# Group 1's operands ahead of the context's, and later turns of the token groups, in a hybrid gated-recurrence and convolution layer

## Chip, cores and metric

The kernel runs on one core of one Trainium2 chip. The metric is the device time of an execution in microseconds. "PE" is TensorE's matmul row, "PEld" its weight loads, "DVE" VectorE, "ACT" ScalarE, "POOL" GpSimd and "SP" SyncE, whose queue issues the DMAs named here. Times are in microseconds from the span's start unless stated otherwise.

## The reference

One layer of a flow-matching generator: batch 1, 2048 tokens and 256 context tokens of width 1024. Cut to what matters:

```python
shift, scale, gate = jnp.split(jax.nn.silu(c) @ w_ada[l] + b_ada[l], 3, axis=-1)
shift_c, scale_c, gate_c = jnp.split(jax.nn.silu(c_ctx) @ w_ada[l] + b_ada[l], 3, axis=-1)
h = rmsnorm(x, norm_w[l]) * (1.0 + scale[:, None]) + shift[:, None]
hc = rmsnorm(xc, norm_w[l]) * (1.0 + scale_c) + shift_c
p = h @ w_in[l]                      # 1024 x 9216 columns
pc = hc @ w_in[l, :, :HG_COLS]
...
qc, vc, kcf, gcf, kcb, gcb = hgrn_prep(pc[..., :HG_COLS], lb_f, lb_b)
oc, s_f, s_b = bidir_scan(qc, kcf, kcb, vc, gcf, gcb, s0, s0)
q, v, kf, gf, kb, gb = hgrn_prep(p[..., :HG_COLS], lb_f, lb_b)
o, _, _ = bidir_scan(q, kf, kb, v, gf, gb, s_f, s_b)
y_hg = hgrn_out(o, p[..., 4 * HG_WIDTH:HG_COLS], hg_onorm_w[l], x.dtype)
y_cv = conv_branch(p[..., HG_COLS:], conv_w[l], grid=True)
y = jnp.concatenate([y_hg, y_cv], axis=-1) @ w_out[l]
x = x + gate[:, None] * y
return rmsnorm(x, final_norm_w)
```

Everything is float32. The context gives only the start states of each head's scan, one per direction.

## The kernel before

**Products.** A float32 operand is split into a high and a low float16 part, and a product takes three matmuls (hi by hi, hi by lo, lo by hi). The input projection works on *units*: a pair of 128-column blocks of `w_in` against one group of 512 tokens (four groups, NG = 4). A normal unit ("head") goes by a scheme of seven block products (`seven`, matmuls at L890 to L892) in place of eight, for which a group needs seven operands, B11, T1, T2, B21, T3, B22 and T4 (`OPS`), made from the rows of h by additions and subtractions. Two kinds of units are simpler: "plain" (L1410 to L1412), for group 0's first use, straight from its rows, and "ctx" (L1396 to L1398), for the 256 context tokens, from the tile `hc`.

**Stretches.** The work runs in stretches, one for each head and group. Head 0 takes the groups in the order 0, 1, 2, 3 (stretches 0 to 3), head 1 in the order 3, 2, 1, 0 (stretches 4 to 7), and so on. Stretch 0 has four plain units and the context's three units of head 0; stretches 1 to 3 have the head units for gates and values and one unit of output gates. In a stretch, `run` issues the matmuls of its units one step (three matmuls) after the other, and between them the other work: the scan of the stretch before (`chain`: levels, key turns, states, outputs) and `extra`. Each piece of that work has a weight, and `merge_steps` spreads the two lists over the stretch's steps by their weights. So the order on every engine is written out by the program, and each engine works its instructions off in that order.

**How a group's operands come to be.** `norm_group` gives a group five lists: loads; squares (L238) and the norm (`rsqrt`, thirteen small DVE instructions, then scaling at L244 on ACT and L246 on DVE); four *turns*; four *late turns*; and `raw`. A turn k transposes blocks k and k + 4 of the normed rows on PE (L253), applies scale and shift on ACT (L274), and in `combine` makes the seven operands' slices: four subtractions on DVE (L328, L329, L331, L337), high parts by `cast` (L281 on ACT, L279 on POOL), low parts on DVE (L298), into "pair" tiles of which there are four, and seven stores on SP (L300) into `Hd`, the group's operands in DRAM. `prefetch` loads an operand back into a "hop" tile (L1297) when a slot is free and the group is said to be ready (`set_ready`); a stretch's first product needs the first of these, hop1B for stretch 1.

**Group 0** is special. Its rows are transposed early, between the products of the modulation (`modulate`, L200), as `raw` rows; when the modulation's result `pada` is there, `modulate_end` copies it (L209), transposes it (L212) and adds the bias, `affine` makes scale and shift for the tokens (m = 0) and the context (m = 1) with one small matmul each (L139), and group 0's rows are scaled (L268, L270), cast (L281) and subtracted (L290) into `plain`. The scaled rows are also stored to `Xd` (L313). Three of group 0's operands are slices of `plain` and are stored by `store_first` (L1333, twelve stores); the other four are made by `late_turn`, which loads rows back from `Xd` (L321).

**When.** The lists are joined at L1445 to L1463. In stretch 0, `early` is the context's norm and turns, then group 1's norm and turns, then group 2's norm and its first turn. Stretch 1 has the other three turns of group 2, then the loads, the norm and the first turn of group 3; stretch 2 has group 3's other three; stretch 3 has group 0's four late turns. The context's scan steps stand in stretch 1.

## Time and profile before

| | us |
|---|---|
| median of 3 runs | 2189.02 (2188.14 to 2189.62) |
| the profiled execution | 2194.8 |
| its span | 2193.0 |
| PE busy | 2095.4 (96%) |
| DVE busy | 1652.7 (75%) |
| ACT busy | 1168.0 (53%) |
| POOL busy | 158.2 (7%) |

The stretches begin, by their first matmul, at 44.7 (stretch 0), 97.0 (1), 154.3 (2), 195.2 (3), 238 (4), 281.9 (5) and 314.9 (6). A row of a timeline has the start, the duration, engine, line, operation and tiles, and in brackets the idle time of the engine before it with what ended it. A row of a window has, for each engine, busy time and the number of instructions; then the granted clock of TensorE, where 1.00 is full speed, the mean busy share of the DMA engines, and GB/s. A row of a group has busy time, the mean in ns, and the idle time before its members.

### The profile page before, as it was taken

The numbers are of one execution on the slowest core, as the hardware profiler recorded it, in microseconds if no ns is written. First come the engines' busy times: TensorE is split into PE (matmuls) and PEld (weight loads), VectorE is DVE, ScalarE is ACT, GpSimd is POOL, SyncE is SP. The second block draws the span as 40 slices with busy tenths as digits, with TensorE's granted clock in tenths as the row PEclk, the third lists the DMA queues.
The fourth block names the chain that finished last, engine by engine and source line by source line (L and its number), as shares of the span: only waits on it lengthen the run. The fifth ranks groups of instructions, "written<-read, shape, count | busy, mean of one in ns | idle before, by whom it ended". The sixth has DMA issues, their size and how long they took to land.

```text
span 2193.0 us, 51887 instructions
## 1 busy us (share of the span) xinstructions
PE 2095.4 (96%) x21563; PEld 1469.7 (67%) x21563; DVE 1652.7 (75%) x3457; ACT 1168.0 (53%) x2340; POOL 158.2 (7%) x239
## 2 busy tenths in 40 slices
PE   5789999999999999999999998999999999999998
PEld 2677788888888888888888887444444444444443
DVE  7887887878769777788687786688778646687775
ACT  7865656656557555575676654354444323333332
POOL 0211100010101110110111100000000000000000
PEclk8999999999999999999999999999999999999999
DMA  9765533342344233423543357933443215633321
GB/s 348 237 210 177 158 99 107 136 136 88 99 140 143 96 112 107 141 97 124 187 152 129 117 183 232 292 106 111 135 139 96 92 32 181 212 118 114 124 88 58
DMA packets 196176, 309.89 MB, mean 141 GB/s; under 512 B 13538, under 2 KB 126562, under 8 KB 194148
## 3 DMA queue, kind: packets, MB, share of 16 engines
q1 hardware_dynamic: 193780, 302.64, 42.2%
q8 instruction: 169, 2.77, 0.5%
q10 hardware_dynamic: 2160, 3.93, 0.5%
q14 instruction: 67, 0.55, 0.1%
HBM read 241.50 MB, written 65.01 MB: 140 GB/s over the span
## 4 chain that ended last, share of the span: by engine, by line
PE 66%; DVE 19%; ACT 7%; DMA 5%; issue 2%; POOL 1%; SPq 0%; POOLq 0%; ACTq 0%; DVEq 0%
PE sa L890 8%; PE sa L892 8%; PE sa L891 8%; PE sb L890 4%; PE sb L891 4%; PE sb L892 4%; PE sa_o L890 2%; PE sa_o L891 2%; PE sa_o L892 2%; DVE e_p L152 2%; PE A L599 2%; PE sc L890 2%; PE sc L892 2%; PE sc L891 2%; DVE Q L460 2%
## 5 line engine op out<-in xcount | busy, mean ns | idle before, releaser
L453 DVE TENSOR_TENSOR K<-K,tot 128x512 f32<-128x512 f32 x192 | 133.6, 696 | 61.8 <-PE A L627 27.6
L890 PEld LDWEIGHTS <-e_p 128*128 128x128 f16 x1368 | 134.3, 98 | 63.1 <-issue 5.2
L891 PEld LDWEIGHTS <-e_p 128*128 128x128 f16 x1368 | 134.5, 98 | 61.6 <-issue 12.3
L892 PEld LDWEIGHTS <-e_p 128*128 128x128 f16 x1368 | 134.5, 98 | 52.9 <-issue 1.5
L460 DVE TENSOR_TENSOR Q<-Q,tot 128x512 f32<-128x512 f32 x192 | 132.4, 690 | 41.4 <-PE A L599 28.0
L569 ACT ACTIVATE km<-K 128x512 f32<-128x512 f32 x160 | 109.0, 686 | 72.1 <-DVE K L453 63.0
L890 PEld LDWEIGHTS <-whib_p 128*128 128x128 f16 x912 | 89.7, 98 | 44.1 <-issue 7.5
L891 PEld LDWEIGHTS <-whib_p 128*128 128x128 f16 x912 | 89.8, 98 | 39.7 <-issue 5.7
L891 PEld LDWEIGHTS <-whia_p 128*128 128x128 f16 x912 | 89.5, 98 | 37.3 <-issue 4.8
L890 PEld LDWEIGHTS <-whia_p 128*128 128x128 f16 x912 | 89.5, 98 | 37.2 <-DMA hop3B<-Hd3B 2.4
L892 PEld LDWEIGHTS <-wlob_p 128*128 128x128 f16 x912 | 89.8, 98 | 35.0 <-issue 0.6
L892 PEld LDWEIGHTS <-wloa_p 128*128 128x128 f16 x912 | 89.6, 98 | 34.6
L151 ACT ACTIVATE e_p<-ws_p,sc_p 128x512 f16<-128x512 f32 x108 | 77.2, 717 | 51.4 <-DVE ws_p L413 32.0
L576 POOL COPY qm<-Q 128x512 f32<-128x512 f32 x64 | 55.6, 869 | 622.0 <-DVE Q L460 619.0
L635 POOL COPY A<-Ac 32x128 f32<-32x128 f32 x128 | 68.4, 534 | 375.0 <-ACT A L631 371.0
L897 ACT ACTIVATE u<-sa,sx_w 128x256 f32<-128x256 f32 (+1 forms) x114 | 59.7, 523 | 58.6 <-PE sa L892 49.0
L897 ACT ACTIVATE p<-sb,sx_w 128x256 f32<-128x256 f32 (+1 forms) x114 | 59.3, 520 | 54.8 <-PE sb L892 54.0
L897 ACT ACTIVATE p<-sa,sx_w 128x256 f32<-128x256 f32 (+1 forms) x114 | 59.0, 517 | 47.1 <-PE sa L892 46.2
L813 ACT ACTIVATE cv<-c,small 128x512 f32<-128x512 f32 (+1 forms) x36 | 24.2, 673 | 105.8 <-DVE c L831 49.9
L152 DVE SCALAR_TENSOR_TENSOR e_p<-ws_p,sc_p,e_p 128x512 f16<-128x512 f32 x108 | 78.7, 748 | 0.4 <-ACT e_p L151 0.4
L378 ACT ACTIVATE junk<-ws_p 128x1024 f16<-128x1024 f32 x72 | 75.6, 1050 | 1.9 <-DMA ws_p<-in_w_in 1.8
L151 ACT ACTIVATE hiS_o<-y_o,sc_y 128x1024 f16<-128x1024 f32 x32 | 36.7, 1148 | 74.3 <-PE sa_o L891 32.1
(865 smaller groups left out, 6978.9 us busy)
## 6 DMA issues: line engine op xcount, KB each, us to landing
ws_p<-in_w_in SPq DMA_DIRECT2D x72, 512.0 KB, 4.3
y_o<-yT SPq DMA_DIRECT2D x32, 512.0 KB, 3.7
xt_x<-in_x SPq DMA_DIRECT2D x16, 512.0 KB, 5.1
wa<-in_w_ada SPq DMA_DIRECT2D x16, 512.0 KB, 10.2
Gd<-zs SPq DMA_DIRECT2D x32, 256.0 KB, 3.6
wos<-in_w_out SPq DMA_DIRECT2D x32, 256.0 KB, 3.8
sg<-Gd SPq DMA_DIRECT2D x32, 256.0 KB, 4.1
yT<-y SPq DMA_DIRECT2D x32, 256.0 KB, 2.2
```

The source lines that it names most:

```text
L151: S.activation(hi, src, AF.Copy, scale=st[:, 0:1])
L152: V.scalar_tensor_tensor(lo, src, st[:, 0:1], hi, ALU.mult, ALU.subtract)
L378: S.activation(junk.rearrange("p (k n) -> p k n", k=KT), stage[i], AF.Abs, accum_out=r)
L453: V.tensor_tensor(m, m, sub(cur, nb + 1, [[2, np_], [-(nb + 1), 2], [0, B]]), ALU.mult)
L460: V.tensor_tensor(m, m, sub(cur, 1, [[2, np_], [nb - 1, 2], [0, B]]), ALU.mult)
L569: S.activation(sub(s.km, 0, [[2 * B, n // (2 * B)], [B, 2], [1, B]]), mix(s.K, n, B, n // (2 * B)), AF.Copy)
L576: G.tensor_copy(sub(qm, 0, [[2 * B, n // (2 * B)], [B, 2], [1, B]]), mix(s.qf, n, B, n // (2 * B)))
L635: G.tensor_copy(A3[js, :, js], s.Ac[js])
L890: PE.matmul(ps, hi[:, k], rh, start=start and k == 0, stop=False, skip_group_check=not start)
L891: PE.matmul(ps, hi[:, k], right(name, 1, k), start=False, stop=False, skip_group_check=not start)
L892: PE.matmul(ps, lo[:, k], rh, start=False, stop=k == nk - 1, skip_group_check=not start)
L897: last_keep.append(S.activation(r, ps, AF.Copy, scale=sx))
```

## The change

- `modulate_end` copies `pada` half on DVE and half on ACT. The last two of group 0's eight `raw` transposes no longer stand ahead of it: they are issued behind its transposes, in banks of another pool, and are copied by ACT. `follow` holds an instruction behind a given one on the same engine.
- Group 1's loads stand ahead of the context's. `affine(1)` comes behind the first three low parts of group 0; a group's squares come behind the last cast, and its norm behind the last low part, of the group named by `before`.
- Stretch 0 keeps only its four plain units. `early` is now an empty step of weight 25.0, group 1's norm and turns, group 0's `store_first`, and group 2's norm. The context's norm and turns (with a third of their weights), its three units and, behind most of the scan of group 0, its scan steps are in stretch 1.
- Stretch 1 has all four turns of group 2 and, behind them, group 3's loads and norm; stretch 2 has all four turns of group 3.
- Group 0's four late turns leave stretch 3: two are in stretch 4 and two in stretch 5.

```diff
     def modulate_end(pada):
         ada_r = ring("ada_r")
-        V.tensor_copy(ada_r, pada)
+        V.tensor_copy(ada_r[:, :HW], pada[:, :HW])
+        S.activation(ada_r[:, HW:], pada[:, HW:], AF.Copy)
...
+    def follow(marks, fn):
+
+        if not marks:
+            return fn()
+        with tc.issue_after(marks[-1].ins):
+            fn()
...
+        before = None if first_ops is not None else "x1" if m else f"x{row0 // GW - 1}"
...
         def square(i):
-            S.activation(junk, xs[i], AF.Square, accum_out=ssq[:, i:i + 1])
+            follow(casts.get(before), lambda: S.activation(junk, xs[i], AF.Square, accum_out=ssq[:, i:i + 1]))
 
         def norm():
+            follow(lows.get(before), scaled)
...
             if wi == 0:
...
-                          (vk, "plain", 1, sg_.value_in), (vk, "plain", 2, sg_.query_in),
-                          (zk, "ctx", 1, lambda ps, w, c_=c_: c_.gate_in(0, ps, w)),
-                          (zk, "ctx", 2, lambda ps, w, c_=c_: c_.gate_in(1, ps, w)), (vk, "ctx", 1, c_.value_in)]
+                          (vk, "plain", 1, sg_.value_in), (vk, "plain", 2, sg_.query_in)]
...
-                if i == 0:
+                if i == 0 or wi == 1:
                     units += [(zk, "ctx", 1, lambda ps, w, c_=c_: c_.gate_in(0, ps, w)),
                               (zk, "ctx", 2, lambda ps, w, c_=c_: c_.gate_in(1, ps, w))]
+                if wi == 1:
+                    units.append((vk, "ctx", 1, c_.value_in))
...
-            chain += scan_steps(heads[pa_h], heads[pa_h].segs[pi])
+            scan = scan_steps(heads[pa_h], heads[pa_h].segs[pi])
+            chain += scan[:-2] + context_steps(h) + scan[-2:] if wi == 1 else scan
...
-    for _, st in ctx_norm[0] + x1_norm[0]:
+    for _, st in x1_norm[0] + ctx_norm[0]:
         st()
-    modulate_end(pada)
+    turned = modulate_end(pada)
+    for k in (KT - 2, KT - 1):
+        follow(turned, first[4][k])
     affine(0, 7)
     for _, st in first[2]:
         st()
-    affine(1, 7)
+    follow(lows["x0"][:3], lambda: affine(1, 7))
...
-            early = (ctx_norm[1] + ctx_norm[2] + n1[1] + n1[2] if wi == 0 else n1[2][1:]) + ready_
+            early = [paced(25.0, lambda: None)] + n1[1] + n1[2] + ready_ if wi == 0 else n1[2] + ready_
             if wi == 0:
                 more_params()
                 for _, st in n2[0]:
                     st()
-                early += [paced(0.1, store_first)]
+                early += [paced(0.1, store_first), paced(0.1, lambda: next_w(1, 6))]
+            if wi == 1:
+                early = [paced(w_ / 3, fn_) for w_, fn_ in ctx_norm[1] + ctx_norm[2]] + early
             if n2 is not None:
-                early += [paced("pause", lambda: None)]
-                if wi == 0:
-                    early += [paced(0.1, lambda: next_w(1, 6))]
-                else:
-                    early += n2[0]
-                early += n2[1] + n2[2][:1]
+                early += ([paced("pause", lambda: None)] + n2[0] if wi else []) + n2[1]
             extra = early + extra
-        elif wi == NG - 1:
-            extra = first[3] + extra
+        elif wi in (NG, NG + 1):
+            extra = first[3][(wi - NG) * 2:(wi - NG) * 2 + 2] + extra
```

On PE, at the end of stretch 0, the last turn of group 1 (its rows are `xt_x_414` and below), the context's products (from `hc`) and the first transposes of group 2 (`xt_x_487` and on) stood ahead of the first product from hop1B. Before:

```order
L253 MATMUL xT_x_951<-ident,xt_x_414 128x128
L1396 MATMUL u_937<-hc,whia_p_218 128x256
...
L1398 MATMUL u_1122<-hc,wloa_p_276 128x256
L253 MATMUL xT_x_1081<-ident,xt_x_487 128x128
...
L253 MATMUL xT_x_1180<-ident,xt_x_489 128x128
L890 MATMUL sa_1163<-hop1B_1012,whia_p_218 128x256
```

At the same place now (group 1's rows end with `xt_x_396`, the context's are `xt_c_398` and `xt_c_400`, group 2's end with `xt_x_494`):

```order
L268 MATMUL xT_x_819<-ident,xt_x_396 128x128
L1425 MATMUL u_796<-hop_2_151,whib_p_277 128x256
...
L535 MATMUL vt_0_952<-ident,vT_0_794 128x128 x4
L902 MATMUL sa_948<-hop1B_874,whia_p_218 128x256
...
L268 MATMUL xT_c_981<-ident,xt_c_398 128x128
...
L268 MATMUL xT_x_1265<-ident,xt_x_494 128x128
...
L1411 MATMUL u_1316<-hc,whia_p_218 128x256
```

The context's transposes and products, and group 2's first transposes, have moved behind hop1B's first product; only plain products and the turn of group 0's values are left between group 1's last turn and it.

On SP, group 0's twelve stores (`Hd0B`) stood together, ahead of the first store of group 1 (`Hd1`). Before:

```order
L1333 DMA Hd0B_90<-hop_3_152 128x2x256 x2
L1333 DMA Hd0B_92<-hop_2_151 128x2x256 x2
L1333 DMA Hd0B_92<-hop_3_152 128x2x256 x2
L370 DMA ws_p_1041<-in_w_in 128x1024
L370 DMA ws_p_1043<-in_w_in 128x1024
L370 DMA ws_p_1045<-in_w_in 128x1024
L300 DMA Hd1T_95<-hpT_x_759 256x1x256
L300 DMA Hd1T_96<-hpT_x_759 256x1x256
```

Now, from group 1's third turn on (the tiles `hpT_x` and `hpB_x` are its pairs):

```order
L315 DMA Hd1T_95<-hpT_x_761 256x1x256
L315 DMA Hd1T_96<-hpT_x_761 256x1x256
L1348 DMA Hd0B_92<-hop_2_151 128x2x256 x2
L315 DMA Hd1B_94<-hpB_x_767 256x1x256
L315 DMA Hd1T_98<-hpB_x_767 256x1x256
L315 DMA Hd1B_97<-hpB_x_772 256x1x256
L315 DMA Hd1B_99<-hpB_x_772 256x1x256
L315 DMA Hd1T_100<-hpT_x_778 256x1x256
L1348 DMA Hd0B_92<-hop_3_152 128x2x256
L315 DMA Hd1T_95<-hpT_x_829 256x1x256
```

Eight of group 0's twelve stores stand between group 1's, and the four weight loads (`ws_p`) have moved behind the last of them, among the hop loads.

Also on SP, the loads of the late turns (`ha_x`, `hb_x` from `Xd`) followed the first hop loads of stretch 5 and the stores of head 0's gates (`Gd`) at the start of stretch 3. Before:

```order
L1297 DMA hop5T_2652<-Hd2T_102 128x2048
L765 DMA Gd_117<-zs_2_2655 128x512
L321 DMA ha_x_2672<-Xd 128x512
L321 DMA hb_x_2673<-Xd 128x512
L321 DMA ha_x_2797<-Xd 128x512
L321 DMA hb_x_2798<-Xd 128x512
L300 DMA Hd0T_88<-hpT_x_2679 256x1x256
```

Now:

```order
L777 DMA Gd_117<-zs_3_3275 128x512
L336 DMA ha_x_3292<-Xd 128x512
L336 DMA hb_x_3293<-Xd 128x512
L794 DMA sg_3_4491<-Gd_116 128x512
L794 DMA sg_2_4953<-Gd_116 128x512
L315 DMA Hd0T_88<-hpT_x_3299 256x1x256
```

They follow the gates of stretch 3's tokens (`zs_3`), a stretch later, and two turns follow another stretch later.

More of the change, by code (lines that the diff above doesn't have):

```diff
@@ L208, in modulate_end @@
         ada_r = ring("ada_r")
-        V.tensor_copy(ada_r, pada)
+        V.tensor_copy(ada_r[:, :HW], pada[:, :HW])
+        S.activation(ada_r[:, HW:], pada[:, HW:], AF.Copy)
         ptr = pa_t("ada_t")
-        for q in range(4):
-            PE.transpose(ptr[:, q * P:(q + 1) * P], ada_r[:, q * P:(q + 1) * P], ident)
+        turned = [PE.transpose(ptr[:, q * P:(q + 1) * P], ada_r[:, q * P:(q + 1) * P], ident) for q in range(4)]
         V.tensor_tensor(ada, ptr.rearrange("p (q j m) -> p j q m", q=4, j=4)[:, :, :, 0:2],
                         sub(bada, 0, [[4, 4], [1, 4], [0, 2]]), ALU.add)
+        return turned
     def affine(m, room):
@@ L229, in norm_group @@
         ssq = sp.tile([P, 16], F32, tag="ssq", name=f"ssq_{nm}", bufs=4)
+        before = None if first_ops is not None else "x1" if m else f"x{row0 // GW - 1}"
+        low, high = lows.setdefault(nm, []), casts.setdefault(nm, [])
         def load(i):
@@ L297, in store2 @@
             cast(eng, hi, row)
-            V.tensor_tensor(lo, row, hi, ALU.subtract)
+            low.append(V.tensor_tensor(lo, row, hi, ALU.subtract))
             for i, op in enumerate(ops):
@@ L343, in norm_group @@
                 [paced("late", lambda k=k: late_turn(k)) for k in range(HK)],
-                [paced(0.0, lambda k=k: raw(k)) for k in range(KT)])
+                [lambda k=k: raw(k, pa_t if k < KT - 2 else px_t) for k in range(KT)])
     class W:
@@ L357, in behind @@
     def behind(fn):
-        if not last_keep:
-            return fn()
-        with tc.issue_after(last_keep[-1].ins):
-            fn()
+        follow(last_keep, fn)
     def load_pair(col0, col1, nm, own=False, a21_at=None):
@@ L1436, in run @@
             pace[1] += 1
-        if wi == 0 and units[-1][1] == "ctx" and len(units) > 2:
+        if wi == 0:
             freed[0] += 5
```

20 lines of the change are left out of this document (11 added, 9 removed).

## The prediction

> **What bounds the kernel now.** I read the page first, then the table of windows cut at the stretches (the first product of stretch 0 and of stretches 1, 2, 3, 4, 5, then the first of stretch 6), then the timelines of PE, ACT, DVE and SP at the seams.
>
> ```profile
> span 2193.0 us, 51887 instructions
> PE 2095.4 (96%) x21563; PEld 1469.7 (67%) x21563; DVE 1652.7 (75%) x3457; ACT 1168.0 (53%) x2340; POOL 158.2 (7%) x239
> ```
>
> TensorE is busy for 96%, so nearly all of the 97.6 us in which it idles is all that an edit of the order can win. The windows say where that idle time lies. Columns: the stretch, its length, then busy time of PE, PEld, DVE, ACT and POOL, the granted clock of PE, DMA share.
>
> ```profile
> core 0: us, PE busy (x) PEld busy (x) DVE busy (x) ACT busy (x) POOL busy (x), PEclk, DMA share, GB/s
> 44.70:97.00 52.30, 41.18 (x322) 33.94 (x322) 43.98 (x115) 45.46 (x79) 13.01 (x20) 0.86 0.79 244
> 97.00:154.30 57.30, 48.12 (x642) 39.58 (x642) 51.31 (x125) 38.24 (x70) 10.41 (x16) 0.94 0.72 240
> 154.30:195.20 40.90, 37.63 (x491) 33.32 (x489) 33.63 (x69) 23.64 (x44) 8.80 (x12) 1.00 0.37 110
> 195.20:238.00 42.80, 37.16 (x502) 29.87 (x503) 31.24 (x66) 24.73 (x48) 7.63 (x10) 0.88 0.66 220
> 238.00:281.90 43.90, 42.16 (x581) 37.03 (x582) 36.07 (x84) 25.12 (x48) 4.40 (x7) 1.00 0.52 164
> 281.90:314.90 33.00, 32.48 (x489) 27.92 (x488) 26.85 (x74) 19.25 (x62) 3.39 (x6) 1.00 0.25 82
> ```
>
> Stretches 0 to 3 leave PE idle for 11.1, 9.2, 3.3 and 5.6 us; stretches 4 and 5 for 1.7 and 0.5. From there on PE is the bound, and the change touches nothing. So the whole effect is what happens between the start of the products and the start of stretch 6 at 314.9 us. The PE timeline has the seams (start, duration, what, in brackets the idle time before it and what ended it):
>
> ```profile
> 36.24 2.10 PE L253 MATMUL xT_x<-ident,xt_x 128*128 128x128 f32 x12
> 39.81 0.63 PE L212 MATMUL ada_t<-ident,ada_r 128*128 128x128 f32 x4 [1.47 <-DVE ada_r L209]
> 41.42 0.31 PE L139 MATMUL ss_h<-rb_h 128*128 128x1 bf16 x2 [0.99 <-DVE rb_h L138]
> 44.74 0.37 PE L1410 MATMUL u<-hop,whia_p 128*128 128x256 f16 x1 [3.01 <-ACT hop L281]
> ...
> 77.37 0.27 PE L1396 MATMUL u<-hc,whia_p 128*128 128x256 f16 x1
> ...
> 81.84 0.27 PE L1398 MATMUL u<-hc,wlob_p 128*128 128x256 f16 x1
> ...
> 94.42 2.42 PE L253 MATMUL xT_x<-ident,xt_x 128*128 128x128 f32 x10 [7.18 <-DVE xt_x L246]
> 97.03 0.37 PE L890 MATMUL sa<-hop1B,whia_p 128*128 128x256 f16 x1 [0.20 <-DMA hop1B<-Hd1B]
> 109.67 0.28 PE L890 MATMUL sa<-hop1T,e_p 128*128 128x256 f16 x1 [3.10 <-ACT h_x L274]
> 195.18 0.28 PE L890 MATMUL sa<-hop3B,whia_p 128*128 128x256 f16 x1 [2.11 <-DMA hop3B<-Hd3B]
> ```
>
> The stall of 7.18 us is put down to x2's scaling, but the row behind it shows the real gate: the first product of stretch 1 needs group 1's operands back from DRAM, and they land at 97.0. The SP timeline shows how they get there, one issue after the other:
>
> ```profile
> 51.62 9.73 SPq L1333 DMA_DIRECT2D Hd0B<-hop  x12
> ...
> 70.90 1.25 SPq L300 DMA_DIRECT2D Hd1T<-hpT_x  x2
> ...
> 74.91 0.56 SPq L300 DMA_DIRECT2D Hd1T<-hpT_x  x1
> ...
> 92.99 0.55 SPq L1297 DMA_DIRECT2D hop1B<-Hd1B  x1
> ```
>
> The first six stores of a turn take from 70.90 to 74.91, 0.67 us each; hop1B lands 4.0 us after its issue.
>
> **Part by part. (A) The start of stretch 1: -8.0 us.** The chain up to group 1's first store, by rows of ACT and DVE:
>
> ```profile
> 43.37 0.80 ACT L270 ACTIVATE h_x<-h_x,ab 128x512 f32<-128x512 f32 x1
> 44.07 0.62 ACT L281 ACTIVATE hop<-h_x 128x512 f16<-128x512 f32 x1
> ...
> 48.27 1.04 ACT L238 ACTIVATE junk<-xt_x 128x1024 f16<-128x1024 f32 x1
> ...
> 67.55 1.47 ACT L274 ACTIVATE h_x<-xT_x,ab 128x512 f32<-128x512 f32 x2
> ```
> ```profile
> 53.98 0.16 DVE L125 TENSOR_SCALAR rsv_x<-ssq_x 128x4 f32<-128x4 f32 x1
> ...
> 56.39 0.75 DVE L246 TENSOR_SCALAR xt_x<-xt_x,rsy_x 128x1024 f32<-128x1024 f32 x1
> ```
>
> Four instead of twelve transposes stand ahead of ada_t, and its copy is halved between DVE and ACT: ada_t at about 38.2 instead of 39.8. Eight transposes (1.4 us at 2.10/12 each) then delay the row sum's matmul, to about 40.2 instead of 41.4; the context's squares no longer stand ahead of L270 on ACT. The first cast ends near 42.2, and plain products start at 42.3, 2.4 us earlier. Eight casts with their scalings take 4.9 us on ACT (43.37 to 48.27), so x1's squares run from 45.8, not after the context's. Four squares at 1.2 end at 50.5, the reciprocal root takes 2.4 (53.98 to 56.39), and ACT scales two of the four tiles between the first unit's evacuations: x1 is ready at 56.5 and its first two turned blocks leave ACT from 56.9. From that point to the first store it is 67.55 to 70.90, 3.35 us: first store at 60.2 instead of 70.9.
>
> But SP now carries group 0's stores between group 1's. Behind that first store and up to hop1B's issue stand 27 more stores of Hd1, 8 of the 12 of Hd0 and one weight load, 37 issues with the first. At 0.67 each that is 24.8 us: hop1B is issued at 85.0 and lands at 89.0, 8.0 us ahead of 97.0. PE finishes the plain products near 72 and waits some 17 us for it. Bounds: at 0.56 (the row at 74.91) 11.9 us ahead; at the 0.81 that the twelve Hd0 stores take each (9.73/12, with their waits) 2.8 ahead. I take 0.67, the pace of the same stores, since turns every 4 us feed SP faster than it issues.
>
> **(B) Stretch 1: +1.7.** It takes over the context: 24 steps of three matmuls, 0.109 each (77.37 to 81.84 is 42 matmuls), 7.8 us, and ten of x2's transposes (1.8). It loses the late hop1T: its slots are free when x1's last turn is done, so the 3.10 us go, with 1.7 us for the half clock behind them. PE busy is 48.1 + 7.8 + 1.8 - 1.7 = 56.0. DVE, by kind:
>
> ```profile
> L298 DVE TENSOR_TENSOR hpB_x<-h_x,hpB_x 128x512 f16<-128x512 f32 x18 | 13.0, 740 | 2.4 <-POOL hpB_x L279 2.2
> L290 DVE TENSOR_TENSOR hc<-h_c,hc 128x256 f16<-128x256 f32 x12 | 4.9, 431 | 1.5 <-POOL hc L279 1.5
> L298 DVE TENSOR_TENSOR hpT_x<-h_x,hpT_x 128x256 f16<-128x256 f32 x9 | 3.8, 420 | 1.2 <-POOL hpT_x L279 1.1
> L328 DVE TENSOR_TENSOR ht_x<-h_x 128x256 f32<-128x256 f32 x9 | 3.8, 419 | 4.8 <-ACT h_x L274 4.8
> L535 DVE TENSOR_TENSOR Q<-q,f 128x1024 f32<-128x1024 f32 x2 | 2.6, 1318 | 0.0
> ```
>
> It gains twelve low parts of 0.43, four differences of 0.42 and group 0's query product of 1.3, 8.2 us. It loses x3's norm (2.4 + 2 x 0.75 = 3.9) and x3's first turn (three of 0.74, one of 0.42, four of 0.42: 4.3), also 8.2. So DVE keeps 51.3 busy, which fills 57.3 at today's 90%. For PE the length is 56.0 if the context's products fill every wait, and 62.1 if the other 6.1 us of idle time stay. I take the middle, 59.0. ACT and POOL lie below both.
>
> **(C) Stretch 2: +2.3.** x3 is now normed and turned four times here instead of three: DVE 33.6 + 4.3 + 3.9 = 41.8 in 40.9 us. The densest window of the transient shows what DVE can do:
>
> ```profile
> 100.00:125.00 25.00, 19.35 (x259) 15.90 (x258) 24.08 (x55) 17.73 (x35) 4.42 (x6) 0.92 0.85 277
> ```
>
> At that 96% it takes 43.5, at 90% 46.7. PE gets 16 transposes more, 37.6 + 2.8 + its 3.3 idle = 43.7, and may wait for hop3B as it does now (2.11). I take 43.2; the ends are 40.9 and 46.7.
>
> **(D) Stretch 3: -5.0.** All four late turns leave it. What they cost there:
>
> ```profile
> 219.90:226.70 6.80, 5.91 (x37) 3.86 (x37) 6.38 (x18) 3.77 (x7) 1.72 (x1) 0.50 0.46 136
> ```
> ```profile
> 220.09 0.37 PE L890 MATMUL sa<-hop3T,e_p 128*128 128x256 f16 x1 [0.91 <-ACT u L897]
> 221.38 0.19 PE L139 MATMUL ss_p<-rb_p 128*128 128x1 bf16 x1 [0.71 <-DVE rb_p L382]
> ```
> ```profile
> 220.03 0.42 DVE L328 TENSOR_TENSOR ht_x<-ha_x 128x256 f32<-128x256 f32 x1 [0.88 <-DMA ha_x<-Xd]
> ```
>
> DVE waits in its queue for Xd to come back, with the evacuations and the row sum of the next weights behind it; PE waits 0.91 and 0.71 for those, and a stretch of 6.8 us at half clock follows, 3.4 us lost: 5.0 together. The least is 1.6 (the waits alone); the most is the whole idle time and both half-clock stretches, 5.6 + 0.12 x 42.8 = 10.7. The hop3B stall remains.
>
> [...]
>
> **(E) Stretches 4 and 5: +2.2.** Each takes two late turns: DVE 0.74 + 6 x 0.42 = 3.3 each, 6.5 a stretch, with four stores and two loads on SP. Stretch 4 has 36.1 + 6.5 = 42.6 of 43.9, at 96% 44.4: +0.5. Stretch 5 has 26.9 + 6.5 = 33.4 of 33.0, at 96% 34.7: +1.7. Nothing (PE hides it) and 4 are the ends. Behind a DVE that waits for Xd stand the same evacuations as in D.
>
> **Sum:** -8.0 + 1.7 + 2.3 - 5.0 + 2.2 = -6.8. The profiled execution took 2194.8 (span 2193.0 and 1.8 around it), so 2188.0 there; the median of the runs is 2189.0, 5.8 lower, and the forecast for it is 2182.2. What this measurement can tell from no change is about 0.2%, 4.4 us.
>
> **The rivals.** *DVE and PE in turn absorb it.* Stretch 1 takes 62.1 (+4.8) and stretch 2 46.7 (+5.8): -8.0 + 4.8 + 5.8 - 5.0 + 2.2 = -0.2, 2188.8. For it: DVE at 96% from 100 to 125, and in-order queues that alternate between the two engines. Against it: the context's products need only hc, and so can run under DVE's waits. Chance 0.18.
>
> *The half clock of stretch 3 stays.* Its cause is not the late turn but short waits that any stretch has: D is -1.6, the sum -3.4, 2185.6. For it: a stretch of half clock also begins after hop3B's 2.11. [...] Chance 0.08.
>
> *The context fills everything.* Stretch 1 takes 56.0 (-1.3), stretches 2, 4 and 5 no more than now: -8.0 - 1.3 - 5.0 = -14.3, 2174.7. For it: PE has 7.8 us more to do where it waited. Chance 0.15.
>
> *SP's queue is the bound, slower.* Group 1's stores share four pair buffers, so a turn's casts wait until the turn before has landed; with group 0's stores in between, and ACT and DVE in order behind such a cast, an issue could cost 1.0 us instead of 0.67. Then hop1B lands at 60.2 + 37 + 4.0 = 101.2, 4.2 later than now, though the context is still to come: +4.2 + 1.7 + 2.3 - 5.0 + 2.2 = +5.4, 2194.4. It decides from about 0.97 an issue. For it: 0.81 for the Hd0 stores. Against it: 0.67 held through each turn. Chance 0.15. That the change does not do what it says can be left out: the order of the queues shows it.
>
> **The numbers.** Forecast 0.44, all of it faster by more than 4.4. Faster: 0.44 + 0.15 = 0.59; within 0.2%: 0.18 + 0.08 = 0.26; slower 0.15. The range goes from 2173 (the third rival, with a little of A's better end) to 2192 (between no change and the slower rival, whose worse half it leaves out).
>
> **What would show it.** Right: plain products from about 42; first Hd1 store near 60, 37 issues at 0.67, hop1B landing near 89 with a PE wait of 15 to 18 us ahead of it; stretch 1 of 57 to 61 us with DVE near 90%; no Xd load and no half clock in the middle of stretch 3. Wrong: hop1B issued after 90 (SP, or a turn that comes late), stretch 1 or 2 longer by over 4 us with DVE above 95%, or waits of several us in stretches 4 and 5 behind Xd.

## The result and the profile after

The changed kernel takes 2196.36 us (median of 6 runs, 2194.36 to 2198.28); the kernel before, on the same chip, 2188.58 (6 runs, 2185.11 to 2189.62). The ratio is 1.0032 [1.0022, 1.0042]: slower by 0.3%, where the prediction had 0.3% faster (2182.2) and its range ended at 2192.0. The profiled execution of after took 2196.59, near its own median. That of before was 6 us above its median, most of it lost between 1835 and 1935 us, where PE idled for 4.2 us (1.4 in after) at a mean clock of 0.98 (1.00); so the two traces differ by only 1.8 us at their ends, but by 8.4 us at the start of stretch 6 (323.3 against 314.9), and it is the second number that agrees with the medians (7.8). A few executions in the runs below took 5892 to 7518 us; the ratios leave them out, and the profiled one of e15 is among them.

The head of the page, after:

```profile
span 2194.8 us, 51871 instructions
PE 2087.4 (95%) x21563; PEld 1465.1 (67%) x21563; DVE 1654.0 (75%) x3456; ACT 1170.8 (53%) x2342; POOL 153.6 (7%) x239
```

The windows of after, cut at the same seams (the first product of stretch 0 and of each stretch to the sixth):

```profile
42.17:91.90 49.73, 28.57 (x229) 23.85 (x228) 37.05 (x103) 37.63 (x60) 7.13 (x12) 0.77 0.71 225
91.90:158.40 66.50, 56.92 (x666) 47.09 (x667) 56.25 (x125) 43.53 (x83) 12.70 (x22) 0.94 0.53 177
158.40:210.10 51.70, 42.41 (x559) 35.61 (x558) 39.24 (x88) 29.49 (x52) 9.40 (x14) 0.97 0.48 155
210.10:245.30 35.20, 33.58 (x504) 28.75 (x505) 25.12 (x50) 23.53 (x44) 3.84 (x6) 1.00 0.44 161
245.30:288.60 43.30, 40.52 (x574) 35.88 (x572) 38.23 (x87) 24.73 (x47) 5.35 (x8) 1.00 0.58 183
288.60:323.30 34.70, 33.47 (x488) 28.06 (x486) 30.58 (x80) 21.82 (x66) 4.25 (x8) 1.00 0.55 169
```

Read it by PE's column. In stretches 0 to 2 together PE does 28.57 + 56.92 + 42.41 = 127.9 us of work, where before it did 41.18 + 48.12 + 37.63 = 126.9: the same. But it idles 21.2 + 9.6 + 9.3 = 40.0 us where it idled 23.6. The change started the products 2.5 us earlier, and by stretch 3 the kernel is 14.9 us late (210.1 against 195.2). Stretch 3 gives 7.6 back (35.2 for 42.8, the clock at 1.00), stretches 4 and 5 take 1.1: 8.4 late.

The largest wait, in PE's timeline of after:

```profile
42.17 0.27 PE L1425 MATMUL u<-hop,whia_p 128*128 128x256 f16 x1 [2.13 <-ACT hop L296]
...
91.91 0.40 PE L902 MATMUL sa<-hop1B,whia_p 128*128 128x256 f16 x1 [18.52 <-DMA hop1B<-Hd1B]
...
210.11 0.28 PE L902 MATMUL sa<-hop3B,whia_p 128*128 128x256 f16 x1 [0.38 <-DMA hop3B<-Hd3B]
```

Before, hop1B was awaited too, but PE had the context's products to do meanwhile; now it stands 18.52 us. The stretch behind the wait, which was to get the context's work into its gaps, is 66.5 us long instead of 57.3.

### The profile page after: what moved, and what is told of

It is laid out like the page before. It is cut to its first block, busy times and chain, and to the rows that moved or that the text cites. A ratio compares the mean times of both kernels' runs of the same rounds, so it can differ in the third digit from the quotient of the medians.

```text
span 2194.8 us, 51871 instructions
## 1 busy us (share of the span) xinstructions
PE 2087.4 (95%) x21563; PEld 1465.1 (67%) x21563; DVE 1654.0 (75%) x3456; ACT 1170.8 (53%) x2342; POOL 153.6 (7%) x239
## 4 chain that ended last, share of the span: by engine, by line
PE 64%; DVE 17%; ACT 6%; DMA 3%; issue 3%; POOL 1%; SPq 0%; POOLq 0%; DVEq 0%; ACTq 0%
PE sa L902 8%; PE sa L904 8%; PE sa L903 8%; PE sb L902 4%; PE sb L903 4%; PE sb L904 4%; PE sa_o L902 2%; PE sa_o L903 2%; PE sa_o L904 2%; DVE e_p L152 2%; PE sc L902 2%; PE sc L904 2%; PE sc L903 2%; PE A L611 2%; DVE Q L472 2%
## 5 line engine op out<-in xcount | busy, mean ns | idle before, releaser
L465 DVE TENSOR_TENSOR K<-K,tot 128x512 f32<-128x512 f32 x192 | 133.0, 692 | 54.5 <-PE A L639 23.6
L151 ACT ACTIVATE e_p<-ws_p,sc_p 128x512 f16<-128x512 f32 x108 | 77.3, 717 | 51.3 <-DVE ws_p L425 30.9
L909 ACT ACTIVATE p<-sa,sx_w 128x256 f32<-128x256 f32 (+1 forms) x114 | 59.0, 518 | 41.8 <-PE sa L904 41.1
```

The lines of the kernel that those rows point to most:

```text
L151: S.activation(hi, src, AF.Copy, scale=st[:, 0:1])
L465: V.tensor_tensor(m, m, sub(cur, nb + 1, [[2, np_], [-(nb + 1), 2], [0, B]]), ALU.mult)
L909: last_keep.append(S.activation(r, ps, AF.Copy, scale=sx))
```

## Experiments

The theories at the start. **Q**: stretches 1 and 2 are long because something comes late in an in-order queue (in e1 x3's last load, in e3 the stores). **W**: they are long because of the work that was moved into them. Each expectation says which work it means: a turn and a norm more (e1, e6), or the context's work, which no longer fills the wait for hop1B (e7). **T** is the first of these: whole turns (of x2 in stretch 1, x3 in stretch 2) are the cost. Kernels are timed against before on the same chip; "after" stands for 2196.4. Edits are given against after, unless they say before.

### e1: x3's loads ahead of the pause

```
-early = ... if wi == 0 else n1[2] + ready_
+early = ... if wi == 0 else n1[2] + (n2[0] if n2 else []) + ready_
```

> The changed kernel with one move: group 3's four loads are written ahead of the step that says group 2 is ready, so that the fourth stands ahead of the hop2 loads on SP instead of behind six of them. Theory Q (a queue): stretch 2 took 51.7 us because ACT's queue stood still for 3.6 us at the square of that fourth row (it landed at 167.2), with the gates of group 2 behind it, so that DVE was busy for 3.5 of 12 us from 158 to 170 and had everything to do afterwards; with the load earlier that wait goes, stretch 2 takes 43 to 46, and the time falls from 2196.4 to 2188 to 2191. Theory W (work): stretch 2 is long because DVE has a fourth turn and a norm more (39.2 busy); it stays at 49 or more and the time within 2 us of 2196.4.

2196.41 against 2189.39, 1.0028 [1.0014, 1.0042]. The last load is issued at 151.65 (156.42 in after) and ACT's wait at x3's fourth square falls. In after, then in e1:

```profile
167.23 1.06 ACT L250 ACTIVATE junk<-xt_x 128x1024 f16<-128x1024 f32 x1 [3.64 <-DMA xt_x<-in_x]
```
```profile
155.82 1.06 ACT L250 ACTIVATE junk<-xt_x 128x1024 f16<-128x1024 f32 x1 [1.01 <-DMA xt_x<-in_x]
```

A wait of 3.64 us fell to 1.01 and the time did not move: Q fell.

### e2: the context in the wait, behind group 1's turns

```
 units (wi == 0): ..., (vk, "plain", 2, sg_.query_in),
+                 (zk, "ctx", 1, ...), (zk, "ctx", 2, ...), (vk, "ctx", 1, c_.value_in)
-early = [paced(25.0, ...)] + n1[1] + n1[2] + ready_
+early = [paced(25.0, ...)] + n1[1] + n1[2] + [paced(w_ / 12, fn_) for w_, fn_ in ctx_norm[1] + ctx_norm[2]] + ready_
 ...
-early += [paced(0.1, store_first), paced(0.1, lambda: next_w(1, 6))]
-if wi == 1: early = [context's norm and turns] + early
+early += [paced(0.1, store_first), paced(0.1, lambda: next_w(1, 6)), paced(24.0, lambda: None)]
```

> The changed kernel with the context's norm, turns and three units put back to the end of stretch 0, but behind group 1's turns. Theory Q: PE's 18.5 us wait for hop1B is where the context belongs; it costs nothing there, hop1B lands at 91 to 93 as now, and stretch 1, without 7.8 us of products and the evacuations of them, falls from 66.5 to 57 to 60: the time falls by 6 to 9, to 2187 to 2190. Theory W: what stretch 1 lacks is time on DVE and ACT, which the context takes from group 1's turns or group 2's norm wherever it stands: hop1B comes later by 4 us or more, or stretch 1 stays over 63, and the time is 2194 to 2198.

2199.93, 1.0046 [1.0032, 1.0060]: slower still. Windows of e2, stretches 0 and 1:

```profile
42.20:100.80 58.60, 41.60 (x326) 34.11 (x326) 43.08 (x114) 39.57 (x70) 12.15 (x20) 0.83 0.78 259
100.80:162.70 61.90, 48.22 (x572) 38.64 (x570) 51.14 (x126) 42.68 (x77) 9.38 (x14) 0.92 0.45 148
```

Stretch 0 took in 13 us of PE work (28.57 to 41.60), and stretch 1 shrank by 4.6; but its first product from hop1B comes 8.9 later. hop1B itself is not late. Its load is issued at 84.91 (86.63 in after), and products from hop1T run from 90.95. What comes late is the context: its norm is held behind group 1's last low part, as in after, so PE stands still until it is through:

```profile
86.05 3.10 PE L268 MATMUL xT_c<-ident,xt_c 128*128 128x128 f32 x12 [13.99 <-DVE xt_c L261]
```

Then the context's products stand in PE's order ahead of hop1B's. Neither expectation's reason held (Q's free wait, W's late hop1B), and this run does not show what the context costs in the wait, as 14 us of the wait went by before the context could start. By stretch 6 its trace is only 0.8 behind after's (324.1, 323.3).

### e3: group 0's second operands stored in stretch 1

```
-early += [paced(0.1, store_first), paced(0.1, lambda: next_w(1, 6))]
+early += [paced(0.1, lambda: next_w(1, 6))]
 ... wi == 1:
+early = [context's norm and turns] + [paced(0.1, store_first)] + early
```

> The changed kernel with group 0's twelve stores moved to stretch 1, behind the hop1 loads. Theory Q: from the first store of group 1 at 62.2 to the issue of hop1B at 86.6 SP issues without a pause, 36 issues at 0.68, and the casts of group 1 wait for pair tiles that its stores free late; without eight of them hop1B is issued 5.4 us earlier and lands at 86 to 88, and the time falls by 2 to 5. Theory W: group 1's turns come no faster from DVE, ACT and PE (the last transposes stand at 68.3, the last low part at 84.1), hop1B lands at 90 or later and the time stays within 2 us of 2196.4.

2196.17, 1.0033 [1.0019, 1.0048]: no change in the median. In the trace three of the twelve stores still come ahead of hop1B, and a weight load more: 33 issues from the first Hd1 store up to hop1B's where after has 37, in 23.7 us instead of 24.4. hop1B's product comes at 89.1 instead of 91.9, and 2.6 us of that are still there at stretch 6 (320.7). But e1, e4, e9 and e13, whose stretch 0 is that of after, have this product at 90.1 to 91.8, and the profiled execution of e3 was 3.5 us under its own median. So neither a gain nor that SP's queue sets the start of stretch 1 is shown (the product fell between the two expectations, 86 to 88 and 90 or later); what is shown is that stretch 1, 67.0 us, got no shorter.

### e4: the late turns back in stretch 3

```
-elif wi in (NG, NG + 1):
-    extra = first[3][(wi - NG) * 2:(wi - NG) * 2 + 2] + extra
+elif wi == NG - 1:
+    extra = first[3] + extra
```

> The changed kernel with group 0's four late turns back in stretch 3. If term D was right in kind (the late turns, their wait for Xd and the half clock after it cost stretch 3), stretch 3 is longer by 5 to 8 us, stretches 4 and 5 shorter by 1 to 2 together, and the time is 2200 to 2203. If the half clock of stretch 3 had another cause, stretch 3 grows by less than 3 and the time is 2195 to 2198.

2202.41, 1.0056 [1.0041, 1.0071], 6.0 slower than after: stretches 3 and 4 together +6.9, stretch 5 -1.8. So moving the late turns gains.

### e5: before with the late turns alone moved

The reverse of e4's edit, made to before.

> The kernel before with one part of the change alone: group 0's late turns leave stretch 3, two are in stretch 4 and two in stretch 5. If this part earns by itself what it cost to take back in the changed kernel (6.0 us between the medians), the time is 2182 to 2185, with stretch 3 at 35 to 38 instead of 42.8 and no half clock from 220 to 227. If the half clock stays in stretch 3, or stretches 4 and 5 pay it back, the time is 2187 or more.

2185.74 against 2188.95, 0.9988 [0.9977, 0.9998]: between the two expectations, with stretch 3 as the first had it. It runs at full clock:

```profile
194.30:230.90 36.60, 35.33 (x521) 30.53 (x522) 27.45 (x60) 24.17 (x45) 3.84 (x6) 1.00 0.40 148
```

### e6: after with the turns shared out as before

```
-n1[2] + ready_                     +n1[2][1:] + ready_
-... + n2[0] if wi else []) + n2[1] +... + n2[0] if wi else []) + n2[1] + n2[2][:1]
```

> The changed kernel with the turns of groups 2 and 3 as before: group 2's first turn at the end of stretch 0, group 3's first turn at the end of stretch 1. Theory W (the fourth turn and the norm are what stretch 2 lacks time for, since the earlier load did not shorten it): stretch 2 falls from 51.7 to 42 to 45, stretch 1 stays within 3 us of 66.5, and the time falls to 2187 to 2191. Rival: the turn only moves, stretches 1 and 2 together stay at 116 to 119, and the time is 2195 to 2198.

2209.45, 1.0093 [1.0078, 1.0108]. Both theories missed. Stretch 1 of e6, and a wait at its start:

```profile
88.50:177.80 89.30, 67.14 (x720) 54.72 (x721) 68.09 (x161) 54.15 (x101) 16.42 (x25) 0.77 0.56 186
```
```profile
106.05 2.27 PE L268 MATMUL xT_c<-ident,xt_c 128*128 128x128 f32 x8 [6.74 <-DVE xt_c L261]
```

x3's norm and first turn are drawn into the stretch that holds the context, while x2's first turn does not leave it (it comes right behind the first product from hop1B): 89.3 us, PE idle for 22.2 of them and at clock 0.77. One more batch of rows in stretch 1 costs more than its work; stretch 2 returns 8.2 (43.5 for 51.7).

### e7: the context back in stretch 0, ahead of group 1

```
 units (wi == 0): as in e2
-early = [paced(25.0, ...)] + n1[1] + n1[2] + ready_
+early = ctx_norm[1] + ctx_norm[2] + n1[1] + n1[2] + ready_
```

(The early start, the whole turns, the holds, the late context scan and the late turns stay; the context is now held behind group 0, `"x0"`, in place of group 1, `"x1"`.)

> The changed kernel with the context where it was before: its norm and turns ahead of group 1's, its three units in stretch 0. The rest of the change stays. Theory W: all of the work that fills the wait for hop1B is worth more than the 5 us by which hop1B comes earlier without it: stretch 1 begins at 94 to 98 and takes 56 to 60 instead of 66.5, stretch 2 stays at 50 to 52, and the time falls to 2190 to 2193. Rival: the order of SP and the held squares delay hop1B to 100 or later, as the context behind group 1's turns did (100.8), and the time is 2196 or more.

2190.18 against 2188.95, 1.0013 [1.0003, 1.0022]: 6.2 us better than after. Stretches 1 and 2 of e7:

```profile
98.70:155.90 57.20, 47.32 (x578) 40.15 (x579) 48.34 (x118) 35.21 (x64) 10.00 (x14) 0.91 0.63 216
155.90:203.10 47.20, 40.28 (x561) 34.74 (x559) 38.71 (x78) 28.82 (x51) 10.82 (x14) 1.00 0.43 133
```

Stretch 1 starts 6.8 later and ends 2.5 earlier than in after, and stretch 2 takes 47.2 instead of 51.7. hop1B's load is issued 8.1 later (94.71 for 86.63), as the context's norm and turns stand ahead of group 1's: in the wait the context's work is cheaper, not free. That is W for the context, with its size.

### e8: e7 and e6 together

> The changed kernel with both undone, the context and the turns of groups 2 and 3: what is left of the change is the halved copy and the early start of the products (2.6 us), the order of group 0's stores, and the late turns in stretches 4 and 5. If the parts add up, it is the kernel before less 6 for the late turns and less 2 to 3 for the early start: stretch 1 from 94 to 95, stretch 3 from 191 to 194, 2179 to 2182. If the early start is lost to the stores between group 1's, stretch 1 begins at 97 or later and the time is 2183 to 2185.

2197.87, 1.0046 [1.0031, 1.0061], where the expectations ended at 2185; stretch 1 64.5, stretch 2 42.9. Without the context in stretch 1 the old share of turns still costs 7.7, where the kernel before has that share and takes 2189: the parts do not add up, and T is not shown by them.

### e9: fewer products of the context

```
+if k in (0, KT - 1):
     PE.matmul(... three of a context step ...)
```

> The changed kernel with 18 of the 24 steps of the context's products left out (the first and the last of each unit's eight remain), so 54 matmuls or 5.9 us of PE's work less in stretch 1; all that DVE, ACT and POOL do for the context is left as it is. If the context costs stretch 1 by TensorE's time, which the waits there do not hide, stretch 1 falls from 66.5 to 60 to 62 and the time from 2196.4 to 2189 to 2192. If it costs by the order of DVE's and ACT's queues (norm, turns, gates of the context between the scan and group 2's turns), stretch 1 stays at 64 or more and the time at 2194 or more.

2178.15 against 2189.04, 0.9953 [0.9938, 0.9968]; this time falls in all eight heads, so only stretch 1 counts:

```profile
90.80:160.10 69.30, 54.21 (x613) 43.61 (x614) 56.44 (x129) 43.60 (x85) 13.60 (x22) 0.87 0.51 173
```

About fifty matmuls fewer than in after, and the stretch is not shorter but 2.8 longer. PE idles 15.1 instead of 9.6 us, and its mean clock is 0.87 instead of 0.94. Of after's 56.92 us of PE, 51.0 should be left without 5.9 us of products; it is 54.21, so by this estimate the lower clock adds 3.2. Without them the stretch would be some 66, no shorter than in after. TensorE's time alone is not what stretch 1 pays.

### e10, e11: before with the late turns and one more part

e10 is e5 with whole turns (`n1[2]` for `n1[2][1:]`, no `n2[2][:1]`). e11 is e5 with the early start: the hunks of the diff in modulate_end, raw and transposed, and the hold of affine(1, 7).

> The kernel before with the late turns moved (2185.7 by itself) and, as the only other part of the change, all four turns of group 2 in stretch 1 and all four of group 3 in stretch 2. If these turns are what lengthens stretch 2 (47.2 in the changed kernel with the context first, 40.1 with the turns as before), stretch 2 takes 46 to 49 here too, stretch 1 stays within 2 us of 56.9, and the time is 2188 to 2192. If it is something else of the change (the held squares, the order of the stores, the place of the context's scan), stretch 2 takes 40 to 43 and the time is 2184 to 2187.

> The kernel before with the late turns moved (2185.7 by itself) and, as the only other part of the change, the early start: the copy of the modulation's result halved between DVE and ACT, the last two raw transposes behind its turns, and the context's scale and shift behind the first three low parts. The first product comes at about 42.2 instead of 44.7. If that carries through, stretch 1 begins at 94.5 to 95.5 and the time is 2182 to 2184.5, the best so far. If the chain of the context and group 1 through ACT takes it back (its squares follow at the same time as before), stretch 1 begins at 96.5 or later and the time is 2185 to 2187.

e10 2183.45, 0.9976 [0.9964, 0.9988]; e11 2182.05, 0.9969 [0.9957, 0.9982], against 2189.04. e11 came as its first theory had it; e10 is below both of its theories, with stretch 2 longer and stretch 1 shorter than either. Stretches 1 and 2 of e10:

```profile
101.20:145.30 44.10, 41.34 (x538) 34.70 (x538) 40.56 (x87) 27.31 (x53) 8.80 (x13) 0.97 0.66 221
145.30:197.80 52.50, 43.72 (x570) 36.61 (x568) 40.12 (x90) 32.59 (x57) 9.06 (x14) 0.97 0.49 157
```

Stretch 2 is as long as in after (51.7), but here stretch 1 has become 44.1. So stretch 2's length is the price of the moved turns, and it is a fair exchange: what stretch 2 gains, stretch 1 loses (the two take 96.6 here, 97.0 in e5). In after stretch 1 was refilled with the context.

### e12: the context's norm in stretch 0

```
-before = None if first_ops is not None else "x1" if m else f"x{row0 // GW - 1}"
+before = None if first_ops is not None or m else f"x{row0 // GW - 1}"
-early = [paced(25.0, ...)] + n1[1] + n1[2] + ready_
+early = [paced(25.0, ...)] + n1[1] + ctx_norm[1] + n1[2] + ready_
```

> The changed kernel with the context's squares and norm taken out of their hold behind group 1 and recorded in stretch 0, right behind group 1's norm; its turns stay in stretch 1's list. Theory C (a chain that starts late): the context's squares stand on ACT at 86.0, behind group 2's, its norm on DVE from 89.8, its first low part at 96.4, so the 18.5 us in which PE waits, and in which DVE is idle for 6 and ACT for 5, cannot be used; with the norm at 57 to 60 the turns fall into that wait, hop1B lands at 91 to 94, stretch 1 falls from 66.5 to 58 to 62 and the time to 2189 to 2193. Theory D (DVE's queue as a whole): the turns then stand ahead of group 1's low parts, hop1B lands at 96 or later, and the time stays at 2194 or more.

2194.65 against 2187.88, 1.0034 [1.0022, 1.0046]; stretch 1 65.8. The theory that the context comes too late in its stretch, behind its own norm, fell: an earlier start returns 0.7 of stretch 1. Its rival's mark, hop1B at 96 or later, was missed too (90.9).

### e13: the context's low parts on POOL

```
-low.append(V.tensor_tensor(lo, src, hi, ALU.subtract))
+low.append((G if m else V).tensor_tensor(lo, src, hi, ALU.subtract))
```

> The changed kernel with the context's twelve low parts on POOL (busy 12.7 of stretch 1's 66.5 us) instead of DVE (56.3 of them); they took DVE 5.6 us there. If DVE's busy time in stretch 1 is what the context costs, stretch 1 falls by 4 to 7, to 60 to 62, and the time to 2190 to 2193. If it is the length of the context's chain (norm, turn, products, gates, scan, each behind the other), POOL's low parts, at least as slow, change nothing or add to it: stretch 1 at 65 to 70, the time 2195 to 2199.

2202.28, 1.0072 [1.0054, 1.0090]. Stretch 1, and the low parts' group in it, of e13; then the group in after:

```profile
90.10:160.60 70.50, 58.47 (x666) 48.15 (x667) 54.09 (x118) 43.81 (x85) 24.81 (x34) 0.92 0.51 171
```
```profile
L305 POOL TENSOR_TENSOR hc<-h_c,hc 128x256 f16<-128x256 f32 x12 | 10.6, 890 | 1.2 <-ACT hc L296 0.7
```
```profile
L305 DVE TENSOR_TENSOR hc<-h_c,hc 128x256 f16<-128x256 f32 x12 | 5.6, 483 | 4.6 <-POOL hc L294 4.6
```

VectorE lost 5.6 us of work and kept 54.1 busy in a stretch 4.0 us longer. POOL takes 890 ns for what VectorE does in 483, on the path to hc: 1.84 times as long. Relieving VectorE alone gives nothing back either, though the slower low parts blur this test.

### e14, e15: early start, whole turns and late turns; and a late context scan

e14 is e11 with e10's edit: after without the holds, the late context scan, the moved context and the new order of the first loads. e15 adds `scan[:-2] + context_steps(h) + scan[-2:]`.

> The kernel before with three parts of the change: the late turns, the early start, and the turns of groups 2 and 3 each whole in its own stretch. The first two gave 2182.1 together. If the parts add up, the turns change it by no more than 2: 2180 to 2184, with stretch 2 at 50 to 53, stretch 1 at 43 to 46. If the turns cost stretch 2 more than they give stretch 1, the time is 2185 or more.

> The kernel of the three parts (late turns, early start, turns whole in their stretches) with one thing more of the change: the context's scan steps stand behind most of group 0's scan in stretch 1 instead of ahead of it. With the context first, the changed kernel stood at 2190.2, the three parts alone at 2180 to 2184: if the place of the scan makes that difference, this takes 2187 to 2191, with stretch 1 or 2 longer by 4 to 7; if it is the held squares and norms or the order of the loads, this stays within 2 of the three parts alone.

e14 2184.30 against 2187.88, 0.9981 [0.9972, 0.9991]; e15 2186.84, 0.9991 [0.9982, 1.0001], just under the 2187 of its theory. Windows of e14, stretches 0 to 2:

```profile
43.00:98.90 55.90, 42.61 (x347) 35.92 (x346) 48.29 (x139) 47.25 (x83) 12.92 (x20) 0.85 0.76 232
98.90:142.30 43.40, 40.33 (x545) 34.04 (x539) 41.35 (x87) 28.59 (x55) 10.74 (x14) 1.00 0.70 236
142.30:195.40 53.10, 46.03 (x571) 37.94 (x570) 40.90 (x90) 32.41 (x57) 9.38 (x14) 0.90 0.47 152
```

This is the comparison that carries the result: e14 and after differ in the place of the context's work, its scan included, and else in the holds and in the order of the first loads and the place of one weight load and a pause in stretch 0, which come to 0 (e16) and -2 us (e7 against e17). With the context out, stretch 0 loses 14.0 us of PE work and 11.2 of VectorE's, and ends 7.0 earlier. With the context in, stretch 1 takes 23.1 longer: PE +16.6 (up to 4.0 of it by the clock, an estimate from 0.94 for 1.00 over 66.5 us), DVE +14.9, PE idle +6.5. Stretch 2 is the same to 1.4. The waits of PE in stretch 1, in after and then in e14 (total, times, longest):

```profile
PE sa L902 <- DMA hop1B<-Hd1B: 18.5, 1, 18.5
PE sa L902 <- DVE vT L913: 2.5, 1, 2.5
PE A L611 <- DVE Q L547: 1.6, 1, 1.6
PE u L1411 <- DVE f L913: 1.3, 1, 1.3
```
```profile
PE A L607 <- DVE Q L468: 0.8, 2, 0.6
PE A L635 <- DVE Q L468: 0.8, 1, 0.8
```

Without the context the two engines hardly wait for each other; with it PE is held by evacuations and query steps that stand on VectorE behind the context's instructions. The query step that ends the wait of 1.6 runs behind two low parts, the evacuation that ends the wait of 2.5 behind steps of the context's scan:

```profile
101.78 0.94 DVE L305 TENSOR_TENSOR hc<-h_c,hc 128x256 f16<-128x256 f32 x2
102.65 1.21 DVE L547 TENSOR_TENSOR Q<-q,f 128x1024 f32<-128x1024 f32 x1
...
140.36 0.21 DVE L478 TENSOR_TENSOR tot_c<-tot_c 128x64 f32<-128x64 f32 x1
140.49 0.47 DVE L913 SCALAR_TENSOR_TENSOR vT<-sc,sx_w,p 128x256 f32<-128x256 f32 x1
```

### e16, e17: the holds, and the holds with the late scan

e16 is e14 with the diff's hunks that put squares and norms behind `follow` (the context's behind group 0); e17 adds the late scan, and stands one edit from e7 (the place of the first loads, a weight load and the pause).

> The kernel of the three parts (late turns, early start, turns whole in their stretches; 2184.3) with one thing more of the change: the squares of a group held behind the last cast of the group before, and its norm behind the last low part (the context's behind group 0's). The context's scan late made 2186.8 of it; the changed kernel with the context first took 2190.2. If the holds make what is left, this takes 2186 to 2189; if they cost nothing, 2183 to 2185.5, and the rest lies with the order of the loads and the pause.

> The three parts with both, the holds and the late scan of the context. What then still differs from the changed kernel with the context first (2190.2) is the order of the first loads, the place of one weight load and a pause of stretch 0. If the parts add up, the time is 2188 to 2191, with stretch 1 at 50 to 58 and stretch 2 at 47 to 53; if those small things carry it, the time is 2184 to 2187.

e16 2184.37 against 2188.97, 0.9977 [0.9968, 0.9986]; e17 2192.27, 1.0016 [1.0007, 1.0025]. The holds cost nothing; on top of them the late scan costs 7.9, and e17 ends 1.3 above its expectation (without them it costs 2.5, e15 against e14, where the intervals overlap). In e16's DVE timeline the context's scan runs while PE waits for hop1B (97.0):

```profile
91.65 0.42 DVE L481 TENSOR_TENSOR tot_c<-f_c 128x256 f32<-128x256 f32 x1
92.10 0.42 DVE L468 TENSOR_TENSOR K_c<-K_c,tot_c 128x256 f32<-128x256 f32 x1
...
96.04 0.15 DVE L481 TENSOR_TENSOR tot_c<-tot_c 128x4 f32<-128x4 f32 x1
```

In e17 it falls into stretch 1. The two stretches, e16's and then e17's:

```profile
97.00:145.10 48.10, 43.61 (x570) 36.97 (x570) 44.26 (x95) 32.74 (x59) 9.44 (x14) 0.96 0.63 215
```
```profile
98.20:156.40 58.20, 47.95 (x577) 40.31 (x578) 48.62 (x119) 35.22 (x64) 9.99 (x14) 0.91 0.62 211
```

4.4 us more of DVE's work and a stretch 10.1 longer, of which stretch 2 returns 5.5 (47.8 for 53.3). This is the same effect a second time, on a smaller piece of the context.

### e18: e11 again

> The late turns and the early start on the kernel before, once more with more rounds, as the best version so far (2182.1, six runs): 2181 to 2184, 0.2 to 0.4% below the kernel before.

2183.00 against 2188.97, 0.9974 [0.9963, 0.9985]. With e11's 0.9969 this is the best version found: 6 to 7 us faster than before, 13 faster than after.

The parts in a row, each kernel with all that stands above it (medians, us; before between 2187.9 and 2189.4 on the chips used):

| part added | kernel | median | ratio to before |
|---|---|---|---|
| late turns to stretches 4 and 5 | e5 | 2185.7 | 0.9988 [0.9977, 0.9998] |
| early start | e11, e18 | 2182.1, 2183.0 | 0.9969 [0.9957, 0.9982], 0.9974 [0.9963, 0.9985] |
| whole turns a stretch later | e14 | 2184.3 | 0.9981 [0.9972, 0.9991] |
| holds | e16 | 2184.4 | 0.9977 [0.9968, 0.9986] |
| late context scan | e17 | 2192.3 | 1.0016 [1.0007, 1.0025] |
| place of loads and pause | e7 | 2190.2 | 1.0013 [1.0003, 1.0022] |
| context's norm, turns and products to stretch 1 | after | 2196.4 | 1.0032 [1.0022, 1.0042] |

Two steps lose what the others gain, and both move the context's work out of the wait for hop1B into stretch 1. Steps between neighbours whose intervals overlap (e11 to e16, e17 to e7) can't be told from nothing; those of e5 and e11 just overlap too, but e18 repeats e11's time.

## Why the prediction was wrong, point by point

**A, the start of stretch 1: right in kind, -5.1 for -8.0.** Plain products start at 42.17 (42.3 forecast). The pace of SP was right: 37 issues from the first Hd1 store up to hop1B's, as the first and last of these rows show, in 24.4 us, 0.66 each (0.67). That the queue alone sets this pace is not shown: in e3 33 issues took 23.7. (At 0.56 an issue the text's bound is 12.1 us ahead, not 11.9.)

```profile
62.23 1.25 SPq L315 DMA_DIRECT2D Hd1T<-hpT_x  x2
...
86.63 0.54 SPq L1310 DMA_DIRECT2D hop1B<-Hd1B  x1
```

The first store is 2.0 late, because ACT's scaling of x1 stands behind the first gate's evacuation:

```profile
54.36 0.69 ACT L508 ACTIVATE f<-u,sx_w 128x512 f32<-128x512 f32 x1 [3.98 <-PE u L1427]
...
55.80 1.13 ACT L259 ACTIVATE xt_x<-xt_x,rsy_x 128x1024 f32<-128x1024 f32 x1
```

And hop1B lands 5.3 us after its issue instead of 4.0. In e1, e4, e9 and e13, with the same stretch 0, stretch 1 starts at 90.1 to 91.8, so this term is -5 to -7. The slower rival, SP at 1.0 us an issue with hop1B at 101.2, did not come: the kernel is slower, but by another mechanism.

**B, stretch 1: the step that failed, +9.2 for +1.7.** PE's busy time was forecast as 56.0 and is 56.92. What failed is the next sentence, that the length lies between 56.0 "if the context's products fill every wait" and 62.1 if the idle time stays, with the middle taken: the stretch is 66.5, past both ends. The waits did not stay at 6.1 and were not filled; PE idles 9.6, as much as before (9.2). And VectorE does 56.25, not 51.3: the tally left out the context's last scaling (0.8) and the first step of its scan (0.6), the groups of after in stretch 1:

```profile
L261 DVE TENSOR_SCALAR xt_c<-xt_c,rsy_c 128x1024 f32<-128x1024 f32 x1 | 0.8, 752 | 0.0
...
L465 DVE TENSOR_TENSOR K_c<-K_c,f_c 128x256 f32<-128x256 f32 x1 | 0.6, 629 | 0.0
```

The low parts take 483 instead of 431 ns (0.6), and the remaining 2.9 are spread over many rows of a stretch that is 9 us longer. The root is a wrong view of what the context was for. The text said that PE would wait some 17 us for hop1B (18.52, right) and still booked A as a gain of 8. Against it, it set only 7.8 us of products and 1.8 of transposes, and let them fill half of PE's gaps; but 14 us of PE work had lost their cover. e14 against after prices that cover: 7.0 won in stretch 0, 23.1 lost in stretch 1.

**C, stretch 2: the second term that failed, +10.8 for +2.3.** It kept PE's idle time at today's 3.3. PE 42.4 and DVE 39.2 busy were near the forecast (PE 40.4 of work, DVE 41.8), but PE idles 9.3. e10 and e14 have the same length (52.5, 53.1) without the moved context, so it belongs to the whole turns; there stretch 1 gives it back. The upper end, 46.7, was too low by 5.

**D, stretch 3: right, -7.6 for -5.0** (ends -1.6 and -10.7). The stall and the half clock went, with a clock of 1.00 in stretch 3 of after and of e5, which has this part alone; e4 shows its worth in time, 6.0. So the rival by which the half clock would stay fell. The cause that the text gave was not quite the right one: it had the half clock follow the waits of 0.91 and 0.71, but these end at 220.09 and 221.38, and the clock is down from 219.8 (last section). It also left out the longer wait just ahead of them, of which 0.7 is left in e5; with it the term would have been about -6:

```profile
218.69 0.27 PE L890 MATMUL sb<-hop3B,e_p 128*128 128x256 f16 x1 [1.55 <-ACT p L897]
```

**E: +1.1 for +2.2.**

**The sum.** Forecast -8.0 + 1.7 + 2.3 - 5.0 + 2.2 = -6.8; measured -5.1 + 9.2 + 10.8 - 7.6 + 1.1 = +8.4. B and C are 16 us off, the other terms 1 in all. The rival "DVE and PE in turn absorb it" came nearest in its mechanism, with the wrong ends: it took PE's idle time as it was (62.1) and a VectorE at 90% (46.7) as the worst that in-order queues do, where stretch 1 runs at 85% on each engine and stretch 2 at 76% of VectorE. That the slower rival's 2194.4 is nearest in number is luck, as its hop1B at 101.2 did not come.

**What stays open.** Which engine sets the pace of stretch 1 once the context is in it: less PE work (e9), less VectorE work (e13) and an earlier start of the context's chain (e12) each return nothing, which speaks against any one of them alone (e13 with less force, as its low parts are slower). That PE and VectorE, each in order, take turns holding the other is an argument from the waits and was not shown by a run that relieves both. Small edits also let the scheduler reorder much more than they say (e6, e8), so single differences of 1 to 2 us are not read here.

## What to carry to other kernels

The work that PE did while it waited for hop1B was cheap there (the context's cost stretch 0 7.0 us in e14, and stretch 1 23.1 in after): before moving such work, write down its full time on every engine as a cost at its new place, and set the wait that it leaves behind against the gain of the transfer that comes earlier. Where two in-order engines are as busy as in stretch 1 of before (PE 84%, VectorE 90%), book added work as work plus new waits, not as filling for the gaps. And test a change of several parts one part at a time: here three of them together made about 4 us (two of these 6 to 7), and the others gave back 12.
